# Splitting the first weights of a decoder trunk one by one, in another order of engines and queues

## The chip, the cores and the metric

The program runs on one core of a Trainium2 chip. The metric is the device time of one execution in microseconds (us). Three runs of the kernel before took 941.19, 941.29 and 944.08 us, so its median is 941.29 us. One further execution was profiled; it took 941.45 us, and its profile spans 939.3 us of that.

## The reference, cut to what matters

The input x has 256 positions of 1024 numbers in float32. Two layers follow; each is a half SwiGLU step, a mixer, and another half SwiGLU step. The mixers, the shared keys and values, and the last norm are not touched by the change and are left out here.

```python
def rmsnorm(x, g):
    y = xf * lax.rsqrt(jnp.mean(xf * xf, axis=-1, keepdims=True) + RMS_EPS)
    return (y * g.astype(jnp.float32)).astype(x.dtype)

def swiglu(h, w_gate, w_up, w_down):
    return (jax.nn.silu(h @ w_gate) * (h @ w_up)) @ w_down

h = x
for layer in range(DEPTH):        # D_MODEL = 1024, D_FF = 2816, SEQ = 256, DEPTH = 2
    h = h + 0.5 * swiglu(rmsnorm(h, ffn1_norm[layer]), ffn1_w_gate[layer], ffn1_w_up[layer], ffn1_w_down[layer])
    ...                           # the mixer, then a second half SwiGLU step
```

The change sits in the first microseconds of the first SwiGLU step of layer 0: the gate and up products of x with the first 512 columns of the two weight matrices.

## The kernel before, in words

**Numbers in two parts.** Every product runs on TensorE (PE) in the chip's float32r type. A float32 number is split into a high part (a copy rounded to float32r) and a low part (the rest). ScalarE (ACT) makes the high part, VectorE (DVE) subtracts it from the source to get the low part. Then three products are summed: high by high, high by low and low by high. For the gate and up products the weight is the stationary side, a block of 128 by 128. The high part of the weight (`wh`) meets both parts of x at once, 512 columns (line 201); its low part (`wl`) meets only the high part of x, 256 columns (line 207).

**x by blocks.** x stands transposed in the tile `hT`, eight blocks of 128 features by 256 positions. `gain` (line 212) multiplies a block by the gains of the norm and splits it with `parts_of` (line 93). The norm's factor for each position is put in later, after the products, so the products need not wait for it. `two_squares` (line 246) squares two blocks on ACT and sums them on DVE.

**The opening** (`opening`, line 515). Eight accumulators hold gate and up for the first four blocks of 128 output columns. For each block k of 128 features of x, the kernel loads 128 rows by 512 columns of gate and of up (256 KB each), splits them (`split`, line 520) and multiplies (`step`, line 526). Block 0 goes in halves of 256 columns, so that the first product can start early: the first halves of gate and up are asked for on the ACT queue ahead of everything (line 120), and the second halves come on the queue of SyncE (SP, line 541). Each queue issues its transfers in the order of the program. The other x and weights come on the SP queue (lines 116 and 546), apart from block 1 of x, which is asked for on the ACT queue behind the first halves. Blocks 1 to 5 are multiplied one at a time; blocks 6 and 7 together, one output block after the other.

**Order of the instructions.** The source is written in the order above; a scheduler then places each engine's instructions. `queued(p)` (line 157) ties the instructions inside it behind those that were put into the table `marks` under p, on the same engine. After the opening come nine pairs of units of 1 MB gate and 1 MB up weights, split in two pieces of 128 by 1024 each by the same two engines (lines 178 and 179), into seven rotating buffers for `wh` and seven for `wl`.

## Time and profile before

| what | value |
| --- | --- |
| median of three runs | 941.29 us |
| profiled execution, its own time | 941.45 us |
| span of its profile | 939.3 us |
| PE busy | 931.9 us, 99% |
| DVE busy | 859.3 us, 91% |
| ACT busy | 660.7 us, 70% |
| POOL busy | 196.8 us, 21% |
| mean granted clock of PE | 0.998 |

Busy time is the time in which an engine had an instruction in work. The span runs from the first to the last instruction. A row of a timeline gives the start, the duration, the engine, the line of the kernel, the operation, the tiles (out, then in), and in square brackets the idle time of the engine just before it with what ended it. Matmuls overlap: a row of 0.39 us with 512 columns is followed by the next one 0.23 us after its start. SPq and ACTq rows are the issue of a transfer by a queue, not the transfer.

### The profile page before, as it was taken

What the parts mean: (1) busy time and instruction counts of PE and PEld (TensorE: products, weight loads), DVE (VectorE), ACT (ScalarE), POOL (GpSimd) and SP (SyncE); (2) the same over time, 40 slices, a digit from 0 to 9 for tenths busy, and PEclk for the clock granted to TensorE, in tenths of its full rate; (3) what the DMA queues carried; (4) which work ended last, traced back from release to release, by engine and by line L of the source; (5) the groups of instructions that cost most, each with busy time, mean ns of one, the idle gap of its engine ahead of it and who ended that gap; (6) DMA issues with size and microseconds to landing.
All of it is one profiled execution on the core that took longest, in us unless ns stands there. A gap on an engine that the chain in (4) does not pass through costs nothing.

```text
span 939.3 us, 15039 instructions
## 1 busy us (share of the span) xinstructions
PE 931.9 (99%) x5222; PEld 808.8 (86%) x5222; DVE 859.3 (91%) x1523; ACT 660.7 (70%) x1165; POOL 196.8 (21%) x211
## 2 busy tenths in 40 slices
PE   9999999999999999999999999999999999999997
PEld 7888888888899888888888888888888988888886
DVE  7999989988989999889989998899889889979887
ACT  7866667767887666667786656787587876657773
POOL 0132100024461401100024320000254623600000
PEclk9999999999999999999999999999999999999999
DMA  9999778988879999858999986799699689997791
GB/s 330 362 355 335 200 278 277 361 263 282 214 175 259 281 365 279 231 170 327 347 324 311 321 253 180 256 331 379 209 361 243 175 241 304 284 245 255 257 364 49
DMA packets 182380, 259.13 MB, mean 276 GB/s; under 512 B 28320, under 2 KB 126368, under 8 KB 178848
## 3 DMA queue, kind: packets, MB, share of 16 engines
q1 hardware_dynamic: 169504, 229.20, 73.3%
q0 software_dynamic: 12224, 28.32, 14.5%
q8 instruction: 41, 0.67, 0.3%
q10 hardware_dynamic: 576, 0.66, 0.2%
q14 instruction: 35, 0.29, 0.1%
HBM read 242.94 MB, written 48.76 MB: 311 GB/s over the span
## 4 chain that ended last, share of the span: by engine, by line
PE 99%; DMA 0%; ACT 0%; issue 0%; SPq 0%; POOLq 0%; DVE 0%; POOL 0%; ACTq 0%
PE f_g L201 17%; PE f_u L201 17%; PE f_u L207 9%; PE f_g L207 9%; PE dn_f_d L190 4%; PE dn_f_d L194 4%; PE dn_f_d L192 4%; PE dn_f_d_m L192 3%; PE dn_f_d_m L190 3%; PE dn_f_d_m L194 3%; PE ot_bo L887 1%; PE ot_ao L887 1%; PE ot_bo L888 1%; PE ot_ao L888 1%; PE ot_bo L889 1%; PE ot_ao L889 1%
## 5 line engine op out<-in xcount | busy, mean ns | idle before, releaser
L201 PE MATMUL f_g<-x_n,wh_f_g 128*128 128x512 f32 x672 | 170.4, 392 | 0.0
L201 PE MATMUL f_u<-x_n,wh_f_u 128*128 128x512 f32 x672 | 168.8, 390 | 0.0
L201 PEld LDWEIGHTS f_u<-x_n,wh_f_u 128*128 128x128 f32 x672 | 126.1, 188 | 26.6
L201 PEld LDWEIGHTS f_g<-x_n,wh_f_g 128*128 128x128 f32 x672 | 123.0, 188 | 23.7
L179 DVE TENSOR_TENSOR wl_f_u<-raw_f_u,wh_f_u 128x1024 fp32r<-128x1024 f32 x84 | 101.5, 1214 | 3.7 <-ACT wh_f_u L178 3.3
L178 ACT ACTIVATE wh_f_u<-raw_f_u 128x1024 fp32r<-128x1024 f32 x84 | 88.0, 1051 | 20.7 <-PE f_g L201 12.6
L179 DVE TENSOR_TENSOR wl_f_g<-raw_f_g,wh_f_g 128x1024 fp32r<-128x1024 f32 x84 | 101.6, 1214 | 0.8 <-ACT wh_f_g L178 0.5
L207 PE MATMUL f_u<-x_n,wl_f_u 128*128 128x256 f32 x672 | 96.7, 283 | 0.0
L207 PE MATMUL f_g<-x_n,wl_f_g 128*128 128x256 f32 x672 | 96.3, 282 | 0.0
L178 ACT ACTIVATE wh_f_g<-raw_f_g 128x1024 fp32r<-128x1024 f32 x84 | 87.0, 1051 | 11.6 <-PE f_u L201 6.4
L207 PEld LDWEIGHTS f_g<-x_n,wl_f_g 128*128 128x128 f32 x672 | 90.7, 191 | 4.0
L207 PEld LDWEIGHTS f_u<-x_n,wl_f_u 128*128 128x128 f32 x672 | 87.6, 192 | 0.0
L303 POOL TENSOR_TENSOR d_n<-w_n,expo 128x8 f32<-128x8 f32 x5 | 11.1, 2223 | 278.5 <-DVE w_n L299 278.5
L648 POOL COPY scrap<-act_f 128x1 f32<-128x1 f32 x19 | 41.3, 2176 | 129.5 <-ACT act_f L100 115.7
L677 POOL DMA_DIRECT2D made_f_d<-made_f_d x44 | 26.4, 643 | 95.4 <-DVE made_f_d L672 25.5
L100 ACT ACTIVATE left<-q_f 128x512 fp32r<-128x512 f32 x35 | 21.9, 626 | 29.8 <-DVE q_f L425 29.6
L980 POOL TENSOR_SCALAR sm_a<-sm_a,ls_a 128x128 f32<-128x128 f32 (+1 forms) x32 | 32.9, 1059 | 29.1 <-ACT sm_a L970 16.2
L480 ACT ACTIVATE g_f<-g_f 128x512 f32<-128x512 f32 x30 | 19.0, 632 | 27.9 <-DVE g_f L479 27.4
L980 POOL TENSOR_SCALAR sm_b<-sm_b,ls_b 128x128 f32<-128x128 f32 (+1 forms) x32 | 32.9, 1046 | 26.9 <-ACT sm_b L970 21.8
L97 DVE TENSOR_TENSOR left<-q_f,left 128x512 fp32r<-128x512 f32 x35 | 23.9, 683 | 14.0 <-ACT left L100 14.0
L100 ACT ACTIVATE act_f<-g_f 128x256 fp32r<-128x256 f32 x60 | 21.6, 407 | 13.3 <-DVE g_f L483 13.3
L414 ACT ACTIVATE u_f<-f_u 128x256 f32<-128x256 f32 x60 | 22.0, 384 | 12.4 <-PE f_u L207 12.3
(785 smaller groups left out, 2485.8 us busy)
## 6 DMA issues: line engine op xcount, KB each, us to landing
raw_f_g<-in_ffn_w_gate_dram SPq DMA_DIRECT2D x42, 1024.0 KB, 9.5
raw_f_u<-in_ffn_w_up_dram SPq DMA_DIRECT2D x42, 1024.0 KB, 8.1
raw_f_d<-in_ffn_w_down_dram SPq DMA_DIRECT2D x17, 1024.0 KB, 6.0
right_f_d<-in_ffn_w_down_dram SPq DMA_DIRECT2D x32, 512.0 KB, 9.9
raw_f_d<-in_ffn_w_down_dram SPq DMA_DIRECT2D x27, 512.0 KB, 4.8
made_f_d<-in_ffn_w_down_dram SPq DMA_DIRECT2D x44, 256.0 KB, 7.7
made_f_d<-made_f_d POOLq DMA_DIRECT2D x44, 256.0 KB, 6.6
right_f_d<-in_ffn_w_down_dram POOLq DMA_DIRECT2D x16, 512.0 KB, 8.6
```

Source lines behind the costliest of these rows:

```text
L97: return first, nc.vector.tensor_sub(lo, src, hi.bitcast(F32))
L100: first = nc.scalar.activation(hi, src, AF.Copy, scale=scale)
L178: nc.scalar.activation(wh, r, AF.Copy)
L179: nc.vector.tensor_sub(wl, r, wh.bitcast(F32))
L190: nc.tensor.matmul(ac, xh, wh, start=first, stop=False)
L192: nc.tensor.matmul(ac, xh, wl, start=False, stop=False)
L194: nc.tensor.matmul(ac, xl, wh, start=False, stop=last)
L201: nc.tensor.matmul(ac, wh, flat(x), start=first and i == 0, stop=False)
L207: nc.tensor.matmul(ac[:, :S], wl, x[:, 0, :], start=False, stop=last and i == len(ws) - 1)
L648: mark = nc.gpsimd.tensor_copy(scrap, latest[-1][:, 0, 0:1].bitcast(F32))
L677: nc.gpsimd.dma_start(self.home[:, j, n], part)
L980: done = nc.gpsimd.tensor_scalar(sm[:, seg], sm[:, seg], ls[:, t:t + 1], None, op0=ALU.mult)
```

## The change

Six edits, all made for the opening.

1. `parts_of` has a flag `turned`; with it, the high part is made on DVE. It is set for block 0 of x in the first norm alone.
2. Block 1 of x is asked for on the SP queue, behind the second halves of block 0's weights and ahead of the weights of block 1.
3. `split` makes the low part piece by piece as it makes the high part: gate and up each on its own for all of blocks 0, 1 and 2. Before, the low part was one instruction for both, and the high part one for both in the second half of block 0 and from block 2 on.
4. `step` runs the gate sums of all its output blocks ahead of the up sums.
5. The first squares are asked for at block 2, ahead of its weights, and not at block 4.
6. The squares are tied behind marks: the first behind the high part of block 2 of x, the second behind the high part of block 2's weights. The table of marks is shared by all norms, and `gain` writes the entry for the first squares in every norm.

```diff
--- before.py
+++ after.py
@@ -90,14 +90,15 @@
     def flat(ap):
         return ap.rearrange("p c n -> p (c n)")
 
-    def parts_of(hi, lo, src, scale=1.0, later=None):
+    def parts_of(hi, lo, src, scale=1.0, later=None, turned=False):
 
         def rest():
             if isinstance(scale, float):
                 return first, nc.vector.tensor_sub(lo, src, hi.bitcast(F32))
             return first, nc.vector.scalar_tensor_tensor(lo, src, scale, hi.bitcast(F32), op0=ALU.mult, op1=ALU.subtract)
 
-        first = nc.scalar.activation(hi, src, AF.Copy, scale=scale)
+        first = (nc.vector.tensor_scalar_mul(hi, src, scale) if turned else
+                 nc.scalar.activation(hi, src, AF.Copy, scale=scale))
         (later or (lambda call: call()))(rest)
         return first
 
@@ -118,7 +119,6 @@
     early = rawp.tile([P, 2, 2, 512], F32, tag="raw", name="raw_0")
     for i, n in enumerate(("gate", "up")):
         nc.scalar.dma_start(early[:, 0, i, :S], a[f"ffn1_w_{n}"][0][:P, :S])
-    load_x(nc.scalar, 1, 2)
     BF16 = mybir.dt.bfloat16
     fill = nc.const_aps.tensor(1.0, [P, 512], BF16)
     busy = trt("busy")
@@ -217,7 +217,7 @@
         else:
             x = xp.tile([P, 2, S], F32R, tag=f"{tag}{k}", name=f"x_{name}_{k}")
         g = gT[:, gi * KD + k:gi * KD + k + 1]
-        parts_of(x[:, 0, :], x[:, 1, :], hT[:, k, :], g)
+        marks["squares", 0 if k == 2 else -k] = [parts_of(x[:, 0, :], x[:, 1, :], hT[:, k, :], g, turned=name == "n0" and k == 0)]
         return x
 
     def by_token(xs):
@@ -246,7 +246,8 @@
         def two_squares(self, k):
 
             sq = atile([P, 2, S], name=f"sq_{self.name}_{k}")
-            nc.scalar.activation(sq, hT[:, k:k + 2, :], AF.Square)
+            with queued(("squares", k)):
+                nc.scalar.activation(sq, hT[:, k:k + 2, :], AF.Square)
             if k:
                 nc.vector.tensor_add(self.two, self.two, sq)
             else:
@@ -520,11 +521,13 @@
             def split(raw, k, cols=slice(0, 512), by=2):
                 wh, wl = parts[k]
                 for i in range(0, 2, by):
-                    nc.scalar.activation(wh[:, i:i + by, cols], raw[:, i:i + by, cols], AF.Copy)
-                nc.vector.tensor_sub(wl[:, :, cols], raw[:, :, cols], wh[:, :, cols].bitcast(F32))
+                    own = slice(i, i + by)
+                    high = nc.scalar.activation(wh[:, own, cols], raw[:, own, cols], AF.Copy)
+                    marks["squares", 2 if k == 2 else -k] = [high]
+                    nc.vector.tensor_sub(wl[:, own, cols], raw[:, own, cols], wh[:, own, cols].bitcast(F32))
 
             def step(fs, *ks):
-                sums = [(i, n) for i in fs for n in range(2)]
+                sums = [(i, n) for n in range(2) for i in fs]
                 wss = [[(wh[:, n, i * P:(i + 1) * P], wl[:, n, i * P:(i + 1) * P]) for wh, wl in parts[ks[0]:ks[-1] + 1]]
                        for i, n in sums]
                 products_t([acs[i][n] for i, n in sums], wss, norm.x[ks[0]:ks[-1] + 1], ks[0] == 0, ks[-1] == KD - 1,
@@ -539,13 +542,16 @@
                 if k == 0:
                     for i, w in enumerate((wg, wu)):
                         nc.sync.dma_start(raw[:, i, S:], w[:P, S:512])
+                    load_x(nc.sync, 1, 2)
                     split(raw, 0, slice(0, S), 1)
-                    split(raw, 0, slice(S, 512))
+                    split(raw, 0, slice(S, 512), 1)
                 else:
                     for i, w in enumerate((wg, wu)):
                         nc.sync.dma_start(raw[:, i], w[k * P:(k + 1) * P, :512])
-                    split(raw, k, by=1 if k == 1 else 2)
-                if k >= KD // 2:
+                    if k == 2:
+                        norm.two_squares(0)
+                    split(raw, k, by=1 if k < 3 else 2)
+                if k > KD // 2:
                     norm.two_squares(2 * k - KD)
                     if k == KD - 1:
                         norm.fold()
```

The rows below are the order in which an engine or a queue has its instructions, without times. First the SP queue at the very start; `gains_hT` is the tile with the gains and x, `raw_88` holds the raw weights of blocks 0 (rows with 256 columns) and 1 (512 columns). Before:

```order
L116 DMA gains_hT<-in_gains_xT_dram 128x312
L541 DMA raw_88<-in_ffn_w_gate_dram 128x256
L541 DMA raw_88<-in_ffn_w_up_dram 128x256
L546 DMA raw_88<-in_ffn_w_gate_dram 128x512
L546 DMA raw_88<-in_ffn_w_up_dram 128x512
L116 DMA gains_hT<-in_gains_xT_dram 128x512
```

Now:

```order
L117 DMA gains_hT<-in_gains_xT_dram 128x312
L544 DMA raw_88<-in_ffn_w_gate_dram 128x256
L544 DMA raw_88<-in_ffn_w_up_dram 128x256
L117 DMA gains_hT<-in_gains_xT_dram 128x256
L550 DMA raw_88<-in_ffn_w_gate_dram 128x512
L550 DMA raw_88<-in_ffn_w_up_dram 128x512
L117 DMA gains_hT<-in_gains_xT_dram 128x512
```

Block 1 of x (128x256) came into the SP queue as its fourth transfer, and every later one stands one place further back.

Second, ACT from its first instructions on; `x_n_0` is the pair of blocks 0 and 1 of x, `wh_0`, `wh_1` and `wh_2` the high parts of the weights of blocks 0, 1 and 2. Before:

```order
L116 DMA gains_hT<-in_gains_xT_dram 128x256
L135 ACT_TABLE_LOAD
L135 ACTIVATE scrap<-expo 128x1
L100 ACTIVATE x_n_0_151<-gains_hT 128x256
L523 ACTIVATE wh_0_148<-raw_88 128x256 x2
L523 ACTIVATE wh_0_148<-raw_88 128x2x256
L100 ACTIVATE x_n_0_151<-gains_hT 128x256
L523 ACTIVATE wh_1_177<-raw_88 128x512 x2
L100 ACTIVATE x_n_2_206<-gains_hT 128x256 x2
L249 ACTIVATE sq_n_0_264<-gains_hT 128x512
L523 ACTIVATE wh_2_203<-raw_202 128x1024
```

Now:

```order
L135 ACT_TABLE_LOAD
L135 ACTIVATE scrap<-expo 128x1
L525 ACTIVATE wh_0_147<-raw_88 128x256 x4
L101 ACTIVATE x_n_0_150<-gains_hT 128x256
L525 ACTIVATE wh_1_180<-raw_88 128x512 x2
L101 ACTIVATE x_n_2_210<-gains_hT 128x256
L250 ACTIVATE sq_n_0_215<-gains_hT 128x512
L525 ACTIVATE wh_2_207<-raw_206 128x512
L101 ACTIVATE x_n_2_210<-gains_hT 128x256
L525 ACTIVATE wh_2_207<-raw_206 128x512
```

The high part of block 0 of x has left ACT (DVE has it as its first large instruction), the second half of block 0's weights is two instructions, and so are the weights of block 2, with block 3 of x between them.

Third, ACT at the start of the second SwiGLU step of layer 0, some 288 us into the run, a place that the diff does not name; `x_n_0` to `x_n_6` are blocks 0 to 7 of x in pairs, `sq_n` their squares. Before:

```order
L100 ACTIVATE x_n_0_3413<-gains_hT 128x256 x2
L249 ACTIVATE sq_n_0_3490<-gains_hT 128x512
L100 ACTIVATE x_n_2_3437<-gains_hT 128x256 x2
L100 ACTIVATE x_n_4_3461<-gains_hT 128x256 x2
L249 ACTIVATE sq_n_2_3492<-gains_hT 128x512
L249 ACTIVATE sq_n_4_3495<-gains_hT 128x512
L178 ACTIVATE wh_f_g_0_3632<-raw_f_g_3630 128x1024
```

Now:

```order
L101 ACTIVATE x_n_0_3419<-gains_hT 128x256 x2
L101 ACTIVATE x_n_2_3443<-gains_hT 128x256 x2
L101 ACTIVATE x_n_4_3467<-gains_hT 128x256 x2
L250 ACTIVATE sq_n_0_3496<-gains_hT 128x512
L250 ACTIVATE sq_n_2_3498<-gains_hT 128x512
L250 ACTIVATE sq_n_4_3501<-gains_hT 128x512
L101 ACTIVATE x_n_6_3491<-gains_hT 128x256 x2
L250 ACTIVATE sq_n_6_3504<-gains_hT 128x512
L178 ACTIVATE wh_f_g_0_3638<-raw_f_g_3636 128x1024
```

The first squares moved behind blocks 2 to 5 of x, and the first weight piece of the next pair behind the last squares.

## The prediction

> **What bounds the kernel now.** I read the page first, for the busy shares and the chain that ended last, then the waits of PE.
>
> ```profile
> span 939.3 us, 15039 instructions
> ...
> PE 99%; DMA 0%; ACT 0%; issue 0%; SPq 0%; POOLq 0%; DVE 0%; POOL 0%; ACTq 0%
> ```
>
> ```profile
> PE busy L126 <- PEq L1367: 0.8, 1, 0.8
> PE f_g L201 <- ACT wh L523: 0.4, 1, 0.4
> PE f_g L201 <- DVE x_n L98: 0.3, 1, 0.3
> ```
>
> PE is the chain, from its first real product to its last, and it waits three times, all in the opening, for 1.5 us in sum. Nothing after the opening can be shortened by an edit to the opening; what the edit can do is let PE begin its unbroken work earlier. So the question is when PE, once started, no longer stops. The timeline of PE shows it.
>
> ```profile
> 4.70 0.47 PE L201 MATMUL f_g<-x_n,wh 128*128 128x512 f32 x1 [0.26 <-DVE x_n L98]
> 5.00 0.39 PE L201 MATMUL f_u<-x_n,wh 128*128 128x512 f32 x1
> ...
> 6.07 0.28 PE L207 MATMUL f_u<-x_n,wl 128*128 128x256 f32 x1
> 6.70 0.50 PE L201 MATMUL f_g<-x_n,wh 128*128 128x512 f32 x1 [0.35 <-ACT wh L523]
> 7.03 0.39 PE L201 MATMUL f_u<-x_n,wh 128*128 128x512 f32 x1
> ...
> 7.96 0.28 PE L207 MATMUL f_g<-x_n,wl 128*128 128x256 f32 x1
> 8.08 0.28 PE L207 MATMUL f_u<-x_n,wl 128*128 128x256 f32 x1
> 8.20 0.39 PE L201 MATMUL f_g<-x_n,wh 128*128 128x512 f32 x1
> 8.43 0.39 PE L201 MATMUL f_u<-x_n,wh 128*128 128x512 f32 x1
> ```
>
> Undisturbed, a line 201 product follows the last one by 0.23 us and a line 207 product by 0.12 us. A half of block 0 is four of each, 4 x 0.23 + 4 x 0.12 = 1.40 us. The first half starts at 4.70, loses 0.07 at 5.00 (0.30 for 0.23) and ends at 6.07 + 0.12 = 6.19. The second waits until 6.70, loses 0.10 at 7.03, and block 1 starts at 8.20. Lost after the start: 0.07 + 0.51 + 0.10 = 0.68 us. From 8.20 the pace is even. What the first products wait for stands in the timelines of ACT and DVE.
>
> ```profile
> 3.54 0.49 ACT L100 ACTIVATE x_n<-gains_hT 128x256 fp32r<-128x256 f32 x1
> 3.94 0.89 ACT L523 ACTIVATE wh<-raw 128x256 fp32r<-128x256 f32 x2
> 6.01 0.63 ACT L523 ACTIVATE wh<-raw 128x512 fp32r<-128x512 f32 x1 [1.19 <-DMA raw<-in_ffn_w_up_dram]
> 6.55 0.49 ACT L100 ACTIVATE x_n<-gains_hT 128x256 fp32r<-128x256 f32 x1
> 6.95 1.14 ACT L523 ACTIVATE wh<-raw 128x512 fp32r<-128x512 f32 x2
> ```
>
> ```profile
> 4.06 0.48 DVE L98 SCALAR_TENSOR_TENSOR x_n<-gains_hT,x_n 128x256 fp32r<-128x256 f32 x1 [3.17 <-ACT x_n L100]
> 4.86 0.69 DVE L524 TENSOR_TENSOR wl<-raw,wh 128x512 fp32r<-128x512 f32 x1 [0.31 <-ACT wh L523]
> 6.68 0.69 DVE L524 TENSOR_TENSOR wl<-raw,wh 128x512 fp32r<-128x512 f32 x1 [1.13 <-ACT wh L523]
> ```
>
> The first product follows x's low part (4.06 + 0.48 = 4.54, then 0.16 to PE). The second half waits on one instruction for gate and up together, which waits for the later of two transfers. The transfers come last, from SP's issues and the answer on transfers issued about 2.1 us.
>
> ```profile
> 1.17 0.42 SPq L541 DMA_DIRECT2D raw<-in_ffn_w_gate_dram  x1
> 1.63 0.43 SPq L541 DMA_DIRECT2D raw<-in_ffn_w_up_dram  x1
> 2.11 0.43 SPq L546 DMA_DIRECT2D raw<-in_ffn_w_gate_dram  x1
> ```
>
> ```profile
> 1.65 0.45 ACTq L116 DMA_DIRECT2D gains_hT<-in_gains_xT_dram  x1
> ```
>
> ```profile
> raw<-in_ffn_w_gate_dram SPq DMA_DIRECT2D x1, 128.0 KB, 3.0
> ```
>
> ```profile
> raw<-in_ffn_w_gate_dram SPq DMA_DIRECT2D x1, 256.0 KB, 4.5
> raw<-in_ffn_w_up_dram SPq DMA_DIRECT2D x1, 128.0 KB, 4.3
> gains_hT<-in_gains_xT_dram ACTq DMA_DIRECT2D x1, 128.0 KB, 4.5
> ```
>
> ```profile
> 2.50:3.00 0.50, 0.50 (x3) 0.22 (x2) 0.00 (x0) 0.50 (x1) 0.45 (x1) 1.00 1.05 369
> ```
>
> Second half of gate: 1.17 + 3.0 = 4.17. Second half of up: 1.63 + 4.3 = 5.93. Block 1 of x: 1.65 + 4.5 = 6.15. Block 1 of gate: 2.11 + 4.5 = 6.61. From landing to ACT's start takes 6.01 - 5.93, about 0.09; from ACT's end (6.64) to PE 0.06. The window row (DMA share 1.05, 369 GB/s) says that the transfers run full by 2.5 us: a landing is set by the bytes ahead of it.
>
> **The change part by part.** I follow PE from its start.
>
> *High part of x on DVE.* DVE can begin when ACT did, 3.54; x has landed and DVE idles until 4.06. The trace has no such instruction with this output. The nearest is the same operation on the same shape:
>
> ```profile
> L1348 DVE TENSOR_SCALAR out<-out,rms x2: 348/351/354, 935.1 to 935.3; 128x256 f32<-128x256 f32 x2
> ```
>
> Bounds are 0.35 (this row) and 0.48 (line 98, which reads two tensors); I take 0.35, being the same operation. High part to 3.89, low part from 3.92 (0.03 behind, as 4.03 to 4.06 before) to 4.40, first product at 4.56 instead of 4.70. ACT is freed, but gains no time on the up half: that ends at 3.94 + 0.89 = 4.83 because its own transfer landed late, and PE took it at 5.00.
>
> [...] With the slower price the first product would come at 4.69 and block 0 end at 4.69 + 2.80 = 7.49, still within the 7.5 that I take for block 1, so the sum stays.
>
> *Gate ahead.* Two gate products now stand ahead of the first up product: 4.56 + 2 x 0.23 = 5.02, past the 5.00 at which up is ready, so the 0.07 goes. The first half ends at 4.56 + 1.40 = 5.96. Its low parts, now one each for gate and up, take 0.41 by the row of that form:
>
> ```profile
> L97 DVE TENSOR_TENSOR act_f<-g_f,act_f 128x256 fp32r<-128x256 f32 x60 | 22.5, 414 | 0.0
> ```
>
> They end near 4.40 + 0.41 = 4.81 and 4.83 + 0.03 + 0.41 = 5.27, ahead of 5.48 and 5.72, when PE reaches them. In the later blocks the products are the same ones in another order, which costs nothing by itself.
>
> *Second half split in two.* Gate landed at 4.17; ACT splits it from 4.83 (0.45, half of the 0.89 for two of that form) to 5.28; PE takes it at 5.96 without waiting. The two gate products give up until 6.42. With its landing unchanged it is ready at 5.93 + 0.09 + 0.45 + 0.06 = 6.53, a wait of 0.11. With block 1 of x out of its way (128 KB at 369 GB/s is 0.36 us) it lands at 5.57 and waits for nothing. Block 0 ends between 5.96 + 1.40 = 7.36 and 7.47.
>
> *Block 1 of x moved to SP.* It and every transfer behind it are issued about 0.45 later than their place before. Landing by bytes, it comes 0.36 behind up, at 5.93 to 6.29. In the early case ACT makes its high part from 6.02 to 6.51 (0.49), DVE the low part 0.03 + 0.48 later, and PE has it at 7.18 (0.16 more). In the late one ACT is at the up half until 6.47, so x's high part ends at 6.96 and PE has it at 7.63. Block 1 of gate has the same bytes ahead of it as before, so it lands at 6.61; ACT adds 0.09 + 0.63 (the 128x512 row), or starts at 6.96 behind the late x; with 0.06, PE has it at 7.39 or 7.65. So block 1 starts between 7.39 and 7.65. I take 7.5, nearer to the early case, since the bytes in front of up do become fewer. Up of block 1 has four gate products, 0.92, as cover.
>
> [...]
>
> *More instructions.* DVE: 0.35, then 4 x 0.41 for 2 x 0.69 (0.26), and in blocks 1 and 2 each 2 x 0.69 for one 128x1024, which takes 1.18 (half of the 2.35 in the next row; 0.40 for both blocks): 1.01 at most, less overlap. Cover: DVE's 0.31 and 1.13 idle in the rows above. ACT: 2 x 0.45 for one of 0.63 in block 0, covered by its 1.19 idle; in block 2 two instructions for one, where gate's piece ends sooner than the single one did and up has 0.92 of cover. If the cover is gone, the low parts come up to 1.01 later; where that would hurt is the narrowest lead of DVE in the first SwiGLU step:
>
> ```profile
> 85.43 2.35 DVE L179 TENSOR_TENSOR wl_f_u<-raw_f_u,wh_f_u 128x1024 fp32r<-128x1024 f32 x2
> ```
>
> ```profile
> 88.43 0.96 PE f_u L207 x8
> ```
>
> The second piece ends at 87.78 and its first product is the fifth, 88.43 + 4 x 0.12 = 88.91: 1.13 of lead. PE coming 0.70 earlier leaves 0.43, without counting that DVE too starts earlier.
>
> *Squares.* In the opening they stay behind ACT work that is not late. At the start of the second SwiGLU steps one ACT instruction of 128x512 (0.63 by the row of that size) moves behind x, which makes x earlier; the weight piece that comes later is the next pair's, wanted only after all products of this pair. Nothing.
>
> *Sum.* 8.20 - 7.50 = 0.70 us, all kept, since PE neither waits nor changes its work behind. 941.45 - 0.70 = 940.75 for the profiled execution, which lay 0.16 over the median of the runs; **940.6 us** against 941.29.
>
> **The rivals.**
>
> *The moved queue place counts (15%).* If a landing follows its issue and not the bytes, block 1 of gate comes at 2.56 + 4.5 = 7.06, ACT to 7.78, PE 7.84. Gain 0.36: 940.9. For it: nearly equal 4.3 to 4.5 for sizes of 128 and 256 KB. Against: the window's full share.
>
> *DVE's lead is used up (10%).* With all 1.01 uncovered, the lead of 1.13 is short by 0.70 + 1.01 - 1.13 = 0.58; PE waits that long once near 88 us. Gain 0.12: 941.2. For it: the window below, 2.1 idle in 77. Against: idle time in the opening.
>
> ```profile
> 23.00:100.00 77.00, 77.00 (x445) 68.03 (x444) 74.91 (x147) 52.94 (x100) 20.31 (x25) 1.00 1.06 343
> ```
>
> *Slower (8%).* The same lead, but the new order of the first step puts a piece of 1.18 behind other rows on DVE as well. Late by 1.01 + 1.18 = 2.19, over the lead by 1.06: PE is that much later than before, 942.4. It decides as soon as DVE is more than 1.13 later than before near 88 us. To pass 0.3% it would take 1.13 + 2.8 = 3.9; no row gives that, only several such places would.
>
> *The split buys nothing (4%).* The first stall merely moves to block 1, if weights land later than before: 941.3.
>
> **How the numbers follow.** The forecast has 63%, and the rivals the rest. This kernel can tell about 0.3% (2.8 us) from no change. PE's whole wait is 1.5 us, so faster by 2.8 has nothing to come from: 1%. Slower by 2.8 needs the third rival several times over: 3%. Same: 96%. The likeliest case, with block 1 between 7.39 and 7.65, has 940.5 to 940.7. The range takes in the rivals up to 942.4 and, downward, block 0 without any wait (7.36, gain 0.84: 940.45) and first landings that vary by an estimated half a microsecond between executions: 939.9 to 942.4.
>
> **What would show it.** Right: the first product near 4.56, the first up product near 5.02 without a gap, the second half at 5.96, block 1 between 7.39 and 7.65, then no wait of PE to the end. Wrong: a wait of PE in front of block 1 on a transfer or x (first rival), a wait on `wl_f_u` near 85 to 88 us (second and third), or a wait of PE in a second SwiGLU step, which would say that the shared marks do cost something.

## The result, and the profile after

The change made the kernel slower: 951.43 us against 941.75 (medians of 7 runs each on one chip), a ratio of 1.0085, 95% interval 1.0055 to 1.0114. (The ratios here and below are estimated from all runs; they are not the quotients of the medians, which would be 1.0103 here.) The prediction was 940.6, range 939.9 to 942.4. The runs of the change lie between 945.8 and 953.4. The profiled execution took 946.19 us and is one of the shortest; its span is 944.1, 4.8 more than before, which is half of the difference of the medians. The page's head and chain:

```profile
span 944.1 us, 15060 instructions
...
PE 96%; DMA 1%; DVE 1%; issue 0%; ACT 0%; POOLq 0%; POOL 0%; ACTq 0%; SPq 0%
```

PE's share of the chain fell from 99% to 96%. The waits of PE (us in total, times, longest) say where:

```profile
PE f_u L207 <- DVE wl_f_u L179: 3.2, 4, 1.7
```

The waits for `f_g` that stood in this list before, all in the opening, are gone, as meant. In their place are four that did not exist, on low parts of weights. The timeline of PE has them in the first SwiGLU step, far behind the opening. First the change, then the kernel before:

```profile
76.16 1.11 PE L207 MATMUL f_g<-x_n,wl_f_g 128*128 128x256 f32 x8
78.98 0.74 PE L207 MATMUL f_u<-x_n,wl_f_u 128*128 128x256 f32 x4 [1.70 <-DVE wl_f_u L179]
80.11 0.74 PE L207 MATMUL f_u<-x_n,wl_f_u 128*128 128x256 f32 x4 [0.39 <-DVE wl_f_u L179]
...
91.95 0.74 PE L207 MATMUL f_u<-x_n,wl_f_u 128*128 128x256 f32 x4 [0.73 <-DVE wl_f_u L179]
93.09 0.74 PE L207 MATMUL f_u<-x_n,wl_f_u 128*128 128x256 f32 x4 [0.39 <-DVE wl_f_u L179]
93.66 2.02 PE L201 MATMUL f_g<-x_n,wh_f_g 128*128 128x512 f32 x8
```

```profile
76.18 1.11 PE L207 MATMUL f_g<-x_n,wl_f_g 128*128 128x256 f32 x8
77.14 1.12 PE L207 MATMUL f_u<-x_n,wl_f_u 128*128 128x256 f32 x8
...
89.23 2.00 PE L201 MATMUL f_g<-x_n,wh_f_g 128*128 128x512 f32 x8
```

The first and the last row are the same products in both. At the first the change is level with before (76.16 and 76.18: in this execution the opening had gained nothing). At the last it is 4.43 behind. Nearly the whole 4.8 is lost in these 18 us. (The rows overlap, so the list of waits, 3.2 in sum, counts less than is lost from start to start.)

What PE waits for at 78.98 is the low part `wl_f_u` of one weight unit. Here is why it is late; DVE and ACT of the change, then DVE and ACT of before:

```profile
72.95 1.23 DVE L179 TENSOR_TENSOR wl_f_g<-raw_f_g,wh_f_g 128x1024 fp32r<-128x1024 f32 x1
77.36 0.42 DVE L97 TENSOR_TENSOR act_f<-act_f,act_f 128x256 fp32r<-128x256 f32 x1 [3.18 <-ACT act_f L101]
77.70 2.35 DVE L179 TENSOR_TENSOR wl_f_u<-raw_f_u,wh_f_u 128x1024 fp32r<-128x1024 f32 x2
```

```profile
74.75 1.06 ACT L178 ACTIVATE wh_f_g<-raw_f_g 128x1024 fp32r<-128x1024 f32 x1 [3.33 <-DMA raw_f_g<-in_ffn_w_gate_dram]
...
75.97 1.05 ACT L178 ACTIVATE wh_f_g<-raw_f_g 128x1024 fp32r<-128x1024 f32 x1
76.92 0.40 ACT L101 ACTIVATE act_f<-act_f 128x256 fp32r<-128x256 f32 x1
```

```profile
71.71 0.42 DVE L97 TENSOR_TENSOR act_f<-act_f,act_f 128x256 fp32r<-128x256 f32 x1
...
73.78 2.35 DVE L179 TENSOR_TENSOR wl_f_u<-raw_f_u,wh_f_u 128x1024 fp32r<-128x1024 f32 x2
```

```profile
69.67 1.04 ACT L178 ACTIVATE wh_f_g<-raw_f_g 128x1024 fp32r<-128x1024 f32 x1
70.69 0.63 ACT L100 ACTIVATE left<-q_f 128x512 fp32r<-128x512 f32 x1
71.23 0.40 ACT L100 ACTIVATE act_f<-act_f 128x256 fp32r<-128x256 f32 x1
71.53 1.05 ACT L178 ACTIVATE wh_f_g<-raw_f_g 128x1024 fp32r<-128x1024 f32 x1
...
76.26 1.06 ACT L178 ACTIVATE wh_f_u<-raw_f_u 128x1024 fp32r<-128x1024 f32 x1 [3.08 <-DMA raw_f_u<-in_ffn_w_up_dram]
```

Each engine takes its rows here in the order in which they stand in its queue. In the change, ACT has both gate pieces of the next pair ahead of the high part of `act_f` (76.92). The first of them waits 3.33 for its transfer, so the high part waits too. DVE has the subtraction for that `act_f` ahead of `wl_f_u`, so `wl_f_u` waits behind it, although the high parts that it subtracts were all made by 69.1. Its two pieces start at 77.70 instead of 73.78: 3.92 later, where before the first of them was ready 2.14 ahead of PE (75.00 and 77.14). Before, `act_f` was done at 71.23, between the two gate pieces. ACT waited for a transfer there too, 3.08 at 76.26, but nothing that DVE needed soon stood behind it.

The order was moved by the scheduler, not by the diff. The rows of ACT with their numbers, before:

```
L178 ACTIVATE wh_f10_g14_0_1077<-raw_f10_g14_1075 128x1024
L100 ACTIVATE left_3_131<-q_f10_9_891 128x512
L100 ACTIVATE act_f10_10_940<-act2_f10_10_938 128x256
L178 ACTIVATE wh_f10_g14_4_1081<-raw_f10_g14_1075 128x1024
```

and in the change (`g14` is the gate unit of the sixth of the nine pairs, whose first blocks are 4, 6, 8 and so on; the expectations below count from nought and call it the fifth. `act_f10_10` is output block 10):

```
L101 ACTIVATE left_3_130<-q_f10_9_897 128x512
L178 ACTIVATE wh_f10_g14_0_1083<-raw_f10_g14_1081 128x1024
L415 ACTIVATE j_f10_g11_1016<-f10_g11_902 128x256
L178 ACTIVATE wh_f10_g14_4_1087<-raw_f10_g14_1081 128x1024
L101 ACTIVATE act_f10_10_946<-act2_f10_10_944 128x256
```

The transfer itself is later too. The SP queue, before and then in the change, each followed by the landing of its last row, the gate unit that ACT waits for (KB, us from issue to landing):

```profile
48.78 3.02 SPq L639 DMA_DIRECT2D right_f_d<-in_ffn_w_down_dram  x1
51.89 8.33 SPq L667 DMA_DIRECT2D made_f_d<-in_ffn_w_down_dram  x4
60.27 0.42 SPq L169 DMA_DIRECT2D raw_f_g<-in_ffn_w_gate_dram  x1
```

```profile
raw_f_g<-in_ffn_w_gate_dram SPq DMA_DIRECT2D x1, 1024.0 KB, 8.3
```

```profile
50.81 9.46 SPq L673 DMA_DIRECT2D made_f_d<-in_ffn_w_down_dram  x4
60.31 0.55 SPq L645 DMA_DIRECT2D right_f_d<-in_ffn_w_down_dram  x1
60.91 0.60 SPq L169 DMA_DIRECT2D raw_f_g<-in_ffn_w_gate_dram  x1
```

```profile
raw_f_g<-in_ffn_w_gate_dram SPq DMA_DIRECT2D x1, 1024.0 KB, 13.8
```

It landed at 68.6 before and lands at 74.7 now. The fourth copy of down weights (`right_f_d`) stands behind the third group of `made_f_d` loads instead of ahead of it; those loads wait for a buffer until near 60 (the longest of SP's waits for `made_f_d` is 6.1 us, 5.9 before), so the copy is asked for only then, just ahead of the gate unit. From 60 to 65 us less is moved than before (last two columns: DMA share, GB/s), before and the change:

```profile
60.00:65.00 5.00, 5.00 (x29) 4.39 (x29) 5.00 (x8) 2.65 (x5) 3.89 (x2) 1.00 0.95 308
```

```profile
60.00:65.00 5.00, 5.00 (x29) 4.39 (x29) 5.00 (x7) 3.66 (x6) 1.79 (x2) 1.00 0.69 209
```

So there were three candidates. **Copy theory:** the copy's place on SP makes transfers late, and that is the loss. **Order theory:** the new rows of ACT and DVE in the first SwiGLU step are enough. **Opening theory:** the loss comes from what was edited, the added instructions and the start of the clock.

### The profile page after: what moved, and what is told of

The parts are those of the page before. It is cut to its first block, busy times and chain, and to the rows that moved or that the text cites. A ratio compares the mean times of both kernels' runs of the same rounds, so it can differ in the third digit from the quotient of the medians.

```text
span 944.1 us, 15060 instructions
## 1 busy us (share of the span) xinstructions
PE 934.1 (99%) x5222; PEld 809.6 (86%) x5222; DVE 860.4 (91%) x1528; ACT 659.3 (70%) x1166; POOL 189.3 (20%) x211
## 4 chain that ended last, share of the span: by engine, by line
PE 96%; DMA 1%; DVE 1%; issue 0%; ACT 0%; POOLq 0%; POOL 0%; ACTq 0%; SPq 0%
PE f_g L201 16%; PE f_u L201 16%; PE f_u L207 9%; PE f_g L207 8%; PE dn_f_d L190 4%; PE dn_f_d L192 4%; PE dn_f_d L194 4%; PE dn_f_d_m L190 3%; PE dn_f_d_m L192 3%; PE dn_f_d_m L194 3%; DMA raw_f_u<-in_ffn_w_up_dram 1%; PE ot_ao L893 1%; PE ot_bo L893 1%; PE ot_bo L894 1%; PE ot_ao L894 1%; PE ot_ao L895 1%
## 5 line engine op out<-in xcount | busy, mean ns | idle before, releaser
L304 POOL TENSOR_TENSOR d_n<-w_n,expo 128x8 f32<-128x8 f32 x5 | 13.2, 2632 | 276.5 <-DVE w_n L300 276.5
L654 POOL COPY scrap<-act_f 128x1 f32<-128x1 f32 x19 | 33.6, 1768 | 127.7 <-ACT act_f L101 106.9
L101 ACT ACTIVATE x_n<-gains_hT 128x256 fp32r<-128x256 f32 x47 | 21.1, 498 | 12.5 <-DVE gains_hT L846 8.2
```

What stands on the lines that cost most here:

```text
L101: nc.scalar.activation(hi, src, AF.Copy, scale=scale))
L654: mark = nc.gpsimd.tensor_copy(scrap, latest[-1][:, 0, 0:1].bitcast(F32))
```

## Experiments

Beside the ratio to the kernel before, measured beside it, each profile is read by one number: how much PE falls behind the profile of before between the 401st and the 501st of its 2816 gate and up products, which is from 76.2 to 93.4 us before. It is called the step's loss. The change has 4.47 there in its first profile. A profile is one execution: those of the copy moved in the kernel before and of the new rows of ACT and DVE alone were the shortest of their runs, those of the second edit alone and of all edits but the second the longest. The ratios also hold a second stretch that varies by itself, told of at the end.

**The copy put back on SP.** Nothing else moves on any engine. `tie` fixes an order in a queue and adds no wait.

```diff
...
+                if len(copied) == 4:
+                    [tie(m, copied[-1]) for m in made_loads[8:12]]
...
```

> The change whole, with one row of the SP queue put back: the fourth copy of down weights (right_f_d, 512 KB) is issued ahead of the third group of made_f_d loads again, as before the change; ACT, DVE, POOL and PE have the change's order unaltered. Copy theory (the copy behind loads that wait for a buffer leaves the transfers idle near 60 us, and then stands in front of the next gate weights, which land at 74.7 instead of 68.6): those weights land before 70 again, PE's waits on low parts of weights in the first SwiGLU step fall from 3.2 us to under 0.5, time 940.5 to 942. Order theory (the new order of rows on ACT and DVE in the first SwiGLU step is enough by itself): PE still waits 3 us or more on wl_f_u, time 945 or more. Opening theory (what is lost is lost by the added instructions and the later clock of the opening): 946 to 953 as the change.

949.79 us, ratio 1.0072 (1.0047 to 1.0097), step's loss 7.72. The gate unit lands at 71.7, not before 70 as the copy theory asked, but 3 us ahead of the change (ACT waits 1.17 for it, until 71.78), and still the time stays. The loss moved one pair on. ACT, DVE, PE:

```profile
88.19 1.06 ACT L178 ACTIVATE wh_f_u<-raw_f_u 128x1024 fp32r<-128x1024 f32 x1 [5.62 <-DMA raw_f_u<-in_ffn_w_up_dram]
89.15 0.61 ACT L101 ACTIVATE left<-q_f 128x512 fp32r<-128x512 f32 x1
```

```profile
89.79 0.69 DVE L97 TENSOR_TENSOR left<-q_f,left 128x512 fp32r<-128x512 f32 x1 [5.75 <-ACT left L101]
...
90.74 1.22 DVE L179 TENSOR_TENSOR wl_f_g<-raw_f_g,wh_f_g 128x1024 fp32r<-128x1024 f32 x1
```

```profile
92.01 1.23 PE L207 MATMUL f_g<-x_n,wl_f_g 128*128 128x256 f32 x4 [4.46 <-DVE wl_f_g L179]
```

It is the same pattern: the high part of `left` behind a weight piece that waits, DVE's `left` behind that, and a low part behind it for which PE waits. The copy theory by itself falls.

**The copy moved behind the loads in the kernel before.**

The last two lines keep the load of `rot` in its place.

```diff
...
+            if len(loads) == 11:
+                tie(loads[-1], copied[-1])
...
+                if len(copied) == 4:
+                    tie(copied[-1], made_loads[11])
...
-    nc.sync.dma_start(rot, a["rot"].rearrange("t p c n -> p t c n"))
+    with tc.issue_after(loads[14].ins):
+        nc.sync.dma_start(rot, a["rot"].rearrange("t p c n -> p t c n"))
```

> The kernel before, opening untouched, with one row of the SP queue moved: the fourth copy of down weights is tied behind the third group of made_f_d loads, and ahead of the next gate weights. On ACT and DVE one pair of neighbouring rows changes places with it. Copy theory: gate weights land some 6 us later near 74, PE waits 3 us or more near 80 and 92 us, time 945 to 953 with a spread of several us between executions. Order theory: rows of ACT and DVE are the old ones but for that pair, so 941 to 942.5. Opening theory: 941.3.

944.69 us, ratio 1.0016 (0.9999 to 1.0033), step's loss 0.14. ACT now waits longer for transfers than the change does:

```profile
78.10 1.06 ACT L180 ACTIVATE wh_f_u<-raw_f_u 128x1024 fp32r<-128x1024 f32 x1 [3.64 <-DMA raw_f_u<-in_ffn_w_up_dram]
...
90.09 1.06 ACT L180 ACTIVATE wh_f_u<-raw_f_u 128x1024 fp32r<-128x1024 f32 x1 [4.95 <-DMA raw_f_u<-in_ffn_w_up_dram]
```

and PE does not wait in the step. Late transfers alone cost little while the old rows stand around them. Two things limit this: the median is 2.2 above what the order theory allowed, and the profile is of the shortest of ten runs, so a loss in the others is not excluded. The gate unit lands at 71.0 here (61.11 + 9.9), 2.4 later than before: that much the copy's place does by itself.

**The second edit alone, and all edits but the second.** Written from the kernel before:

```diff
-    load_x(nc.scalar, 1, 2)
...
+                    load_x(nc.sync, 1, 2)
```

> The second edit alone: block 1 of x asked for on the SP queue. It gives the SP queue the change's order behind the opening (third pair's gate ahead of the first made_f_d loads, fourth copy behind the third ones), and ACT the change's rows there. Copy theory: 945 to 953. Order theory: the same. Opening theory (DVE's added instructions): 941.3, since none is added here.

949.16 us, ratio 1.0062 (1.0039 to 1.0085), step's loss 5.35. The other kernel has every edit except these two lines:

> All edits but the second: block 1 of x stays on the ACT queue. The SP queue keeps the old order behind the opening; ACT and DVE have a third order of their own in the first SwiGLU step. Copy theory: no wait of PE behind the opening over 0.5 us, 940.5 to 941.8. Order theory: any reshuffled ACT order may cost, 942 to 946. Opening theory: 946 to 953, since DVE's added instructions are all here.

941.54 us, ratio 0.9992 (0.9977 to 1.0007), step's loss 0.00. So the added instructions on DVE and ACT, the gate sums ahead and the moved squares cost nothing. What costs is the moved request for 128 KB at 1.6 us, and it costs near 80 us, through the order that the scheduler then chooses. All edits but the second have an order of their own on ACT and DVE, neither the old one nor the change's, so not every new order costs.

**Old order under the new opening, new order under the old opening.** The instructions behind the opening are created in the same order in both kernels, so a table of positions can tie them, on each engine, into either schedule:

```diff
...
+        for engine, table in tables.items():
+            own = [i for i in made if str(i.engine).endswith(engine)]
+            for early, late in zip(table, table[1:]):
+                tc.add_manual_dep(own[late], own[early].name, ...)
...
```

All edits, old rows of ACT, DVE and SP:

> All six edits, but the rows of ACT, DVE and SP for the pairs of the first SwiGLU step behind the opening tied into the order that they had before the change. Order theory (a high part of left or act_f stands on ACT behind a weight piece that waits for its transfer, DVE's subtraction of it stands ahead of low parts whose sources are ready, and PE waits for those): no wait of PE over 0.5 us behind the opening, no stretch with a clock under 0.99 there, time 940.5 to 941.8. Opening theory (the added instructions and the later clock of the opening cost what was lost): 946 to 953. Copy theory has fallen with the run that put the copy back.

942.7 us, ratio 0.9997 (0.998 to 1.0014), step's loss 0.00. The median is 0.9 over the expected range; the kernel before, measured beside it, had 942.83. The old opening, new rows on all three:

> The kernel before with its opening as it was; only the rows of ACT, DVE and SP for the pairs of the first SwiGLU step are tied into the order that the change gave them. PE's order is the old one to the last row. Order theory: waits of PE on low parts of weights between 75 and 95 us, 3 to 5 us in sum, 946 to 953. Opening theory: 941.3 to 942.

948.56 us, ratio 1.0041 (1.0018 to 1.0063), step's loss 4.95. PE waits on the same low part as in the change:

```profile
79.84 1.71 PE L228 MATMUL f_u<-x_n,wl_f_u 128*128 128x256 f32 x5 [2.21 <-DVE wl_f_u L200]
```

This settles it for the order and against the opening theory: the order carries the loss with it, whichever opening stands ahead.

**ACT and DVE apart from SP.** The old opening and the old SP order, with the new rows of ACT and DVE alone:

> As the last, but SP keeps its old order too, so that only rows of ACT and DVE stand as the change has them. Order theory with ACT and DVE alone at fault: 946 to 953, as with SP's rows moved. If SP's order is a needed part (transfers must be late too, so that the weight pieces on ACT wait): 941.3 to 943.

950.27 us, ratio 1.007 (1.0048 to 1.0092), step's loss 2.90, in the shortest of its nine runs (944.61). PE's waits there (us in total, times, longest):

```profile
PE f_u L228 <- DVE wl_f_u L200: 1.9, 4, 0.9
```

The gate unit lands at 74.1 (61.28 + 12.8) although SP has its old order. So most of the 6 us by which it is late in the change comes with the rows of ACT and DVE and not with the copy's place, which by itself gave 2.4. The converse, all edits and the new SP order with the old rows of ACT and DVE:

> All six edits and the change's SP order, but ACT and DVE have the rows of before in the first SwiGLU step; it differs from the run with the old order on all three in two places of SP alone. Loop theory (the new rows of ACT and DVE are needed for the loss; the SP order only makes transfers later): no wait of PE over 0.6 us behind the opening in the profile, 941 to 944, with ACT waiting for transfers 1 to 4 us as the run before the change with the copy behind did. If SP's order loses time by itself under any rows: 945 to 951.

945.73 us, ratio 1.002 (0.9998 to 1.0042), step's loss 1.18. The median is above what the loop theory allowed and within the other theory's range, and two waits remain, 0.27 and 0.39 near 89 us. So the four corners are:

| rows of ACT and DVE | SP order | median | kernel before, beside it | ratio |
| --- | --- | --- | --- | --- |
| old | old | 942.70 | 942.83 | 0.9997 |
| old | new | 945.73 | 943.03 | 1.0020 |
| new | old | 950.27 | 942.83 | 1.0070 |
| new | new | 949.41 | 942.83 | 1.0071 |

The rows of ACT and DVE are enough for the whole loss. SP's order costs perhaps 2.7 us by the medians under the old rows (1.9 by the ratio, whose interval reaches just below 1), and adds nothing visible to the new ones. The third row has the old opening, the others the new one. The last row is the change itself, run again:

> The change unaltered, for a second profile. Its executions lie between 945.8 and 953.4, and the profiled one was among the shortest. If the longer ones are the same waits followed by a lower clock: PE's waits of 3 to 5 us between 75 and 95 us, and a stretch of some 5 to 10 us behind one of them with a granted clock well under 1, worth the difference to 944. If not: more or longer waits at full clock. Opening: the record of full clock starts at another moment than the 6.24 us of the first profile if that start varies by itself, at 6.24 again if the opening's work sets it.

Its profile (span 946.8) has one longer wait, and a slower clock behind it. PE, then the window behind the wait (length; busy us of PE, PEld, DVE, ACT and POOL; granted clock; DMA share; GB/s):

```profile
79.92 2.36 PE L207 MATMUL f_u<-x_n,wl_f_u 128*128 128x256 f32 x8 [3.42 <-DVE wl_f_u L179]
```

```profile
79.92:83.33 3.41, 3.41 (x12) 2.98 (x13) 3.41 (x6) 0.95 (x3) 1.15 (x3) 0.53 1.12 297
```

Step's loss 5.43: 3.42 of wait, and 3.41 us at half clock, which is 1.7; the other 0.3 was not traced. So part of the spread of the change is the clock: a wait of this size is paid half again. The first seven runs fit: the two shortest have a mean granted clock of 0.999 and 0.998, the five others 0.994 to 0.997.

**Mending single rows.** If the pattern is right, moving the two high parts ahead should end it (the remarks in the code are for the reader):

```diff
+    tie(('f10_g14', 0), ('f10', 'act', 10))    # gate piece behind the high part of act_f
+    tie(('f10_u16', 0), ('left', 'f10_11'))    # up piece behind the high part of left
```

> The change whole, with two rows of ACT moved in the first SwiGLU step: the high part of act_f of output block 10 goes ahead of the first gate piece of the fifth pair, and the high part of left of blocks 10 and 11 ahead of the first up piece of the sixth. PE and SP keep the change's order; DVE changes one pair of neighbouring rows at each place. Row theory (these two high parts, queued on ACT behind a weight piece that waits for its transfer, hold DVE and then PE): ACT may wait for transfers as long as before, but DVE's waits on act_f and left fall under 0.6 us, PE's on low parts under 0.5 us, no low clock behind the opening, 941 to 943. Transfer theory (the late landings do it, whatever stands behind them): PE waits 2 us or more still, 946 to 951.

951.23 us, ratio 1.0094 (1.0063 to 1.0125), step's loss 7.60: a miss. The wait near 80 us did go, but a new one came at the next row of the same kind, which I had left where it was:

```profile
86.08 1.06 ACT L178 ACTIVATE wh_f_g<-raw_f_g 128x1024 fp32r<-128x1024 f32 x1 [3.50 <-DMA raw_f_g<-in_ffn_w_gate_dram]
87.04 0.40 ACT L101 ACTIVATE act_f<-act_f 128x256 fp32r<-128x256 f32 x1
```

```profile
89.83 0.80 PE L207 MATMUL f_g<-x_n,wl_f_g 128*128 128x256 f32 x4 [2.71 <-DVE wl_f_g L179]
```

With only the first of the two ties:

> Only the first of the two rows is moved: act_f of block 10 ahead of the first gate piece of the fifth pair. left of blocks 10 and 11 still stands behind the up piece. Row theory: the wait of PE near 80 us goes, one near 92 us of 0.5 to 4.5 us stays (the run with the copy ahead had 4.46 there, the two profiles of the change 1.1 and none), so 942 to 948, between the change and the run with both rows moved. Transfer theory: 946 to 951.

954.04 us, ratio 1.0112 (1.009 to 1.0134), step's loss 10.98, again a miss: no wait near 80 us, and two of 3.04 and 3.72 at 90.6 and 95.1, at block 11's `act_f` and at `left`. Mending one row makes the sum worse. That is no proof of the row theory, so all rows of the kind from block 10 on were tied, with ten ties: the two above, these, and the same for blocks 13 to 16:

```diff
+    tie(('f10_g16', 0), ('f10', 'act', 11))
...
+    tie(('f10_g16', 0), ('f10', 'act', 12))
...
```

> The change whole, with ten ties on ACT where two were tied before: from block 10 on, the high parts of act_f and left go ahead of the first weight piece of a later pair that stood in front of them. SP and PE keep the change's order. Row theory, wider form (any high part that DVE needs, queued behind any weight piece that waits for a transfer): with two rows tied the wait of PE near 80 us went and one of 2.71 us came at act_f of block 11, behind the next gate piece; with that row and its followers tied too, DVE waits for no act_f or left over 1 us, PE waits under 1 us in sum behind the opening, 941 to 944. If lateness of the transfers decides: PE waits 2 us or more again, on a piece that is itself late (ACT's split ends after PE wants it), 946 to 953.

946.91 us, ratio 1.0038 (1.0019 to 1.0056), step's loss 3.36: less than half of the loss of the two-row kernel, and less than the 4.47 and 5.43 of the change, but over the 944 of the row theory, so a miss as well. DVE waits for no `act_f` or `left` any more; one wait over 1 us is left (3.18 on a factor of the gate, `j_f_g`, that stands on ACT behind an up piece which waits 3.31). PE's 2.47 us of waits are not on a piece that is itself late, which was the sign of the other theory: the high parts of the gate piece that it waits for were made by 77.8, and PE waits until 89.4. Then the ten ties and the copy put back on SP together, two edits shown above:

> The change whole with the ten ties on ACT and the fourth copy back ahead of the third made_f_d loads on SP. If rest and rows are two separate parts of one loss: the late landing of the fifth pair's gate (75.81 with the ten ties) comes back to 69 to 72, PE waits under 0.6 us behind the opening, 941 to 943.5. If the copy's place is nothing and the rest lies in DVE's new rows, which are not mended here: PE waits 1 to 3 us near 80 to 92, 945 to 948 as with the ten ties alone.

943.99 us, 0.5 over the expected range, ratio 1.0013 (0.9994 to 1.0031), step's loss 0.00. PE does not wait in the step, while ACT still waits for transfers:

```profile
76.81 1.06 ACT L178 ACTIVATE wh_f_u<-raw_f_u 128x1024 fp32r<-128x1024 f32 x1 [1.95 <-DMA raw_f_u<-in_ffn_w_up_dram]
...
89.02 1.06 ACT L178 ACTIVATE wh_f_u<-raw_f_u 128x1024 fp32r<-128x1024 f32 x1 [2.88 <-DMA raw_f_u<-in_ffn_w_up_dram]
```

The copy's place, which was worth nothing alone (1.0085 and 1.0071 against 1.0072), is worth the rest here (a step's loss of 3.36 to 0.00; the intervals of 1.0038 and 1.0013 overlap). In these profiles the loss comes where a late transfer meets a row that hands it on; a run with the new rows and no late transfer is missing. Under the change's rows there are enough of either that taking one away only moves the place. No version was measurably faster than the kernel before.

## Why the prediction was wrong, point by point

*First product at 4.56, from the high part on DVE at 0.35:* right. The nine profiles with all six edits have it at 4.37 to 4.54, and the instruction took 0.35, the lower bound that was chosen.

```profile
3.47 0.35 DVE L100 TENSOR_SCALAR x_n<-gains_hT 128x256 fp32r<-128x256 f32 x1 [2.58 <-DMA gains_hT<-in_gains_xT_dram]
```

*First up product without a gap, second half at 5.96 without a wait, block 1 between 7.39 and 7.65:* right as a mechanism, off in size. The second half never waits for its weights. Block 1 starts at 7.38, 7.41 and 7.51 in three of the nine, at 7.74 to 7.83 in four (in two of these PE waits 0.2 to 0.3 for block 1's gate, the first rival), at 8.18 and 8.31 in two. The mean is 7.77; the four profiles with the old opening have 7.97 to 8.43, mean 8.16. By these means the term came to about 0.4 instead of 0.70. What the sum lacked is the pace of PE. Two executions of the change, the shorter run's profile first, then the one taken again:

```profile
4.49 1.19 PE L201 MATMUL f_g<-x_n,wh 128*128 128x512 f32 x2
5.48 0.98 PE L201 MATMUL f_u<-x_n,wh 128*128 128x512 f32 x2
6.30 0.40 PE L207 MATMUL f_g<-x_n,wl 128*128 128x256 f32 x2
```

```profile
4.37 0.87 PE L201 MATMUL f_g<-x_n,wh 128*128 128x512 f32 x2
5.08 0.62 PE L201 MATMUL f_u<-x_n,wh 128*128 128x512 f32 x2
5.53 0.40 PE L207 MATMUL f_g<-x_n,wl 128*128 128x256 f32 x2
```

In the first, two up products take 6.30 - 5.48 = 0.82; in the second 5.53 - 5.08 = 0.45, which is the prediction's 0.23 for each. The trace's clock records begin full clock at 6.24 us in the first and at 4.65 in the second. With the old opening they begin at 3.95, 4.00, 4.80 and 6.56, so the moment is not the edits' doing. PE began 1.75 us ahead of full clock in the first of these two (4.49 and 6.24), 0.28 ahead in the second (4.37 and 4.65), and before 0.75 behind it (4.70 and 3.95): where full clock comes late, an earlier start of PE lies in the slow stretch. The prediction quoted one execution in which the clock came early and took its pace as given. Its range lets the first landings vary by half a microsecond, for which no run is named; what these profiles show to vary is the start of full clock.

*More instructions on DVE and ACT cost nothing, squares cost nothing:* right. With all of them in place the step's loss is 0.00 (all edits but the second, and all edits with the old rows), and PE is as far behind at the end of the second SwiGLU step of layer 0 as at its start (4.50 us, the change's first profile).

*"All kept, since PE neither waits nor changes its work behind":* this step failed. PE's own order hardly changed; the rows of ACT and DVE between 25 and 120 us and those of SP between 30 and 61 us did. Listings of the order, of the start and of 288 us, stood ahead of the prediction, and its third rival even named "the new order of the first step", but priced it as one piece of 1.18 behind other rows, work added on DVE. What the runs showed is not work but waiting: a row that waits for a transfer hands its wait to the rows behind it, and from ACT to DVE to PE (3.33, 3.18 and 1.70 us in the change's first profile). The row to price it by stood in the profile before and was not quoted: ACT waiting 3.08 us at 76.26 for `raw_f_u`. Whatever a new order puts behind such a row may come up to 3 us later, over the lead of 1.13 that the prediction had worked out, and several such rows follow each other. (The lead was even smaller, 0.96: the row at 88.43 is of the chain and begins where the product before it ends; in the timeline the fifth product starts at 88.75.) That passing 0.3% would take DVE 3.9 later, which no row gives, was wrong too: `wl_f_u` came 3.92 later at 77.70, and DVE's waits on `act_f` and `left` in the first profile were 3.18 and 1.26; in the second one of 4.9 was on `act_f`.

*The sign by which the prediction would be wrong* (a wait on `wl_f_u` near 85 to 88 us, for the second and third rival) came, at 79 and 92 us. The *first rival* (the moved request's place in the queue) shows in three of the nine profiles, as waits of 0.2 to 0.6 us on weights of block 1; in one of them block 1 starts at 7.83, where that rival had 7.84. The *fourth* did not appear, as the gain of about 0.4 shows.

**What stays open.** How much each single row of ACT or DVE is worth was not found out, nor ACT's rows apart from DVE's: they act together, and taking one away moved the wait. The step's loss is 2.9 to 7.7 us in the profiles with the change's rows, and in four of the six it is below what the ratio of the same kernel stands for (4 to 8 us in all); the rest was not traced run by run. Why DVE's new rows make the next transfers later even under SP's old order (230 GB/s between 60 and 70 us in that run, 328 for all edits but the second) is only argued: before, SP waits for DVE's `wl_f_g` 23.2 us in sum between 40 and 100 us, so raw buffers seem to come free when DVE has subtracted from them, and a late DVE also delays the loads.

## What to carry to other kernels

Where a scheduler sets the order, price the edit by the whole list of moved rows, not by the place of the diff: a transfer request moved at 1.6 us cost 6 to 7 us, of which 5.35 in its profile by way of rows near 80 us. In the profile before, look for every engine that waits for transfers even though PE does not; whatever a new order put behind such a row in the same queue inherited its wait here (ACT's 3.33 us for the gate piece became DVE's 3.18 for `act_f`). Tie the short instructions that another engine needs (here the high parts of `act_f` and `left`) ahead of the long ones that wait for memory, in the source, so that a change elsewhere cannot shuffle them; tie all of them, since one or two ties left the loss as large or larger here and ten still left 3.36, and look after the order of the transfers too.

## What was not expected of the hardware

**Half clock followed short waits.** In the first SwiGLU step, single waits of PE of 2.21, 2.29 and 3.42 us were each followed by 3.41 us at half clock, one of 4.46 by 6.83 (from before its end on), 2.71 and 1.27 close together by 6.83, 3.04 and 3.72 by 10.24; waits of up to 1.70 by none. The window behind the wait of 2.21 (new order, old opening) has a granted clock of 0.50:

```profile
79.90:83.31 3.41, 3.41 (x12) 2.88 (x13) 3.41 (x7) 1.36 (x4) 1.15 (x3) 0.50 1.11 345
```

These lengths are 3.41 us and its multiples, and so is the one stretch of full clock that the traces of before and of the change's first profile have: it lasts 931.839 us from 3.958 on and 935.252 us from 6.246 on, 273 and 274 times 3.4133, and half clock follows it in both, behind PE's last product. The start of full clock differs between executions by up to 2.6 us (3.95 to 6.56 above); what sets it was not shown.

What counts seems to be PE's idle time within one window. Cut into windows of 3.41 us from each execution's start of full clock on, the first SwiGLU step has six windows at full clock with 2.21 to 3.24 us of idle PE, and half clock follows each; the largest idle time that it does not follow is 1.67. The wait of 4.46 lies across two windows, 2.26 and 2.20, and cost two; the 1.70 and 0.39 of the change's first profile divide into 0.65 and 1.44 and cost none. Later in the run less was enough: 2.12 at 893 us (second edit alone), and in the second mixer 1.62 there and 1.16 in the two-row kernel, while 1.42 was not. So the idle time is not the whole rule.

**A second place that varies by itself.** Between the last product of the third SwiGLU step and the first of the fourth (593 to 757 us before) the profiles of all kernels lose between 0 and 5.9 us against the profile of before: 3.3 for all edits but the second, 3.6 for the ten ties with the copy back, 0.0 for the change's first profile. PE's waits there are on tiles of the second mixer (`qk_b`, `nm_b`; 0.2 to 2.3 us), and with the largest of them, for the second edit alone, half clock came too, as it did in the two-row kernel with waits of 0.4, 0.5 and 0.2. The kernel before ran from 941.2 to 948.6 us over all its runs, so this place is probably its spread as well, though its one profile lost nothing there. It is probably also why the ratios above are uncertain by some 0.2%, and it is why the step's loss was read apart.
